# Cast order and block 0's gates in the opening, and the last P4 readout, of a fast-matrix-product ReGLU MLP

## The chip, the core and the metric

The kernel runs on one core of a Trainium2 chip. The metric is the device time of one execution in microseconds (us), median of several runs. TensorE (PE) multiplies, VectorE (DVE) and ScalarE (ACT) read its results out of PSUM and convert types, GpSimd (POOL) adds in SBUF, and DMAs are issued from the queues of SyncE (SP), POOL and ACT.

## The reference

```python
batch, seq, dim, hidden = 16, 256, 512, 2048
def reference(x, w1, w2):              # x [16,256,512], w1 [512,4096], w2 [2048,512], float32
    h = x @ w1
    gate, value = np.split(h, 2, axis=-1)
    h = np.maximum(gate, 0) * value
    return (h @ w2).astype(np.float32)
```

## The kernel before

**Tiling.** The 4096 rows of x are four sets of 1024 tokens; `w1` is 16 blocks of 128 hidden columns, each with a gate and a value part. All matmuls take float16 operands and add up in float32 in PSUM. The first product of a block is done by a scheme with seven products in place of eight (class `Block`, P1 to P7, two 512-wide matmuls each), on sums of blocks of x (`x_S1` to `x_S4`) and of `w1` (`wt`) that DVE and POOL make. The second product (`mm2_stream`) has the same seven steps for each of four groups `b` of 128 tokens per half set, eight 256-wide matmuls a step; it is woven into the next set's first product, and the last set's stands alone at the end. Its P4 ends a group: ACT reads 256 columns of the PSUM tile `Y` into the first half of `o2` (L333; the profile calls the tile `pv`), whose second half DVE wrote at P7 (L327), and a DMA carries them to the output (L337). In the last set, groups 2 and 3 send the two halves by DMAs of their own; P4's half goes out from the ACT queue for group 2 and from SP for group 3, the last of all.

**The opening (L417 to L486).** In set 0 the first three blocks are computed without the scheme, by class `Plain`: four accumulated matmuls (e = 0 to 3 over the 512 input columns) for a gate and four for a value. `whole[0..2]` are those blocks for the first 512 tokens, `parts` for the second 512 in two pieces of 256; `lead` is block 3, the first with the scheme. SP loads, in this order: two halves of the first tokens' x (`xf`), the weights of blocks 0 and 1 (all gates, then all values, `fetch_wl`), half of the next tokens (`xg`), block 2's gate weights, block 2's value weights, and the other half of `xg`. In the profile the float32 landing places carry the names of the tiles they borrow: x is `g_S`, the weights are `g`.

All waits come from the tile framework; the order on each engine is the program's order. PE runs `idle(NWARM)`, that is eight 512-wide matmuls on zeros (L177), then transposes x by `turn_pair` (L382; eight 128-wide ones a call). Of the two PSUM tiles of a call DVE copies one and ACT the other into `x_A` as float16 (L384). `cast_w(jb, g_)` (L397 to L400) casts one block's gate or value weights to float16 in `wr`, in two instructions: ACT takes e = 0, 1 and DVE e = 2, 3. The casts of block 0's gate weights stand between the two `turn_pair` calls in the program, so on ACT and DVE they are ahead of the copies of the second call. Block 0's gates are taken as two runs of four 256-wide matmuls, `gates((0,))` and `gates((1,))`, the first of which needs only the first 256 tokens.

For each block `close()` follows `values()`: ACT scales the value out of PSUM (L269), DVE multiplies it with the gate (L270). The second 512 tokens are cast to float16 by DVE in two instructions (L458 and L468, 1024 columns each), transposed on PE in float16 by `turn_half` (L390), and copied by DVE (L391). `cast_w(2, 0)` and `cast_w(2, 1)` are block 2's, at L462 and L465.

Of the kernel before, what the change touches and what calls it, by code (L numbers as in the profile page):

```python
# [11 lines left out]
MAX, MULT = mybir.AluOpType.max, mybir.AluOpType.mult  # L12
LE, GE, LT, ABS_MAX = (getattr(mybir.AluOpType, n) for n in ("is_le", "is_ge", "is_lt", "abs_max"))
COPY, SQUARE = mybir.ActivationFunctionType.Copy, mybir.ActivationFunctionType.Square
ENG = mybir.EngineType

P = 128
TH = 512
PERIOD = 7
NWARM = 8  # L20
NFILL = 1
NPLAIN = 3
HIGH, LOW = 512.0, 32.0
GS = 2.0 ** -19
SLOT = {"P1": 0, "P5": 1, "P2": 3, "P6": 4, "P3": 5, "P7": 9, "P4": 13}
HALF = 256
# [3 lines left out]
@with_exitstack  # L30
def kernel(ctx: ExitStack, tc: tile.TileContext, x, w1, w2, out):

    nc = tc.nc
    x2 = x.flatten_outer_dims()
    out2 = out.flatten_outer_dims()  # L40
    flagpool = ctx.enter_context(tc.tile_pool(name="flagpool", bufs=1))
    flag = flagpool.tile([1, 1], dt.int32, name="flag")
    with ExitStack() as fast:
        unfit = fast_way(fast, tc, x2, w1, w2, out2, flag)
    with tc.If(unfit > 0, label="general"):
        with ExitStack() as general:
            general_way(general, tc, x2, w1, w2, out2)
# [52 lines left out]
def fast_way(ctx, tc, x2, w1, w2, out2, flag):  # L100

    nc = tc.nc
# [7 lines left out]
    NB = TH // P  # L110
# [17 lines left out]
    place = {jb + i: (c, i) for c, (jb, n) in enumerate(CHUNKS) for i in range(n)}  # L128
    wr = [wpool.tile([P, 4, 2, n * P], F16, name=f"wr{c}") for c, (_, n) in enumerate(CHUNKS)]
# [44 lines left out]
    def idle(n):  # L174
        for _ in range(n):
            t = psy.tile([P, TH], F32, name="Y", tag="Y")
            nc.tensor.matmul(t, warm_b[:, :P], warm_b[:, :TH], start=True, stop=True)  # L177
# [106 lines left out]
    def mm2_stream(s, go):  # L284
        last = s == NS - 1
        S = {}

        def mm(name, b, ps, fresh):
            vn, gn = WX[name]
            for k in range(NHC):  # L290
                nc.tensor.matmul(ps, go[gn][:, k, b * P:(b + 1) * P], V[vn][:, k, :], start=fresh and k == 0,  # L291
                                 stop=k == NHC - 1, skip_group_check=True)
                if k < NHC - 1:
                    yield

        def take(pool, nm):
            return pool.tile([P, TH], F32, name=nm, tag=nm)[:, :HALF]

        def step(name, b):
            d = S.setdefault(b, {})  # L300
            if name == "P1":
                d["X"] = take(psx, "X")
                yield from mm("P1", b, d["X"], True)
                d["Y"] = take(psy, "Y")
                nc.scalar.copy(out=d["Y"], in_=d["X"])
            elif name == "P5":
                d["W"] = take(psw, "W")
                yield from mm("P5", b, d["W"], True)
                t = tmp.tile([P, 2, TH], F32, name="pv", tag="tmp")
                d["pu"], d["o2"] = t[:, 0].rearrange("p (a n) -> p a n", a=2), t[:, 1]  # L310
                nc.scalar.activation(d["pu"][:, 0], d["W"], COPY, scale=1 / GS)
            elif name == "P2":
                yield from mm("P2", b, d["X"], False)
                d["o1"] = tmp.tile([P, DO], F32, name="o", tag="o", bufs=4)
                nc.scalar.activation(d["o1"][:, :HALF], d["X"], COPY, scale=1 / GS)
            elif name == "P6":
                yield from mm("P6", b, d["Y"], False)
                nc.scalar.activation(d["pu"][:, 1], d["Y"], COPY, scale=-1 / GS)
            elif name == "P3":
                yield from mm("P3", b, d["W"], False)  # L320
                nc.vector.scalar_tensor_tensor(out=d["o1"][:, HALF:], in0=d["W"], scalar=1 / GS, in1=d["pu"][:, 1],  # L321
                                               op0=MULT, op1=ADD)
                for n in (slice(0, HALF), slice(HALF, DO)) if last and b >= 2 else (slice(0, DO),):
                    nc.sync.dma_start(out=out_v[s, 0, b, :, n], in_=d["o1"][:, n])
            elif name == "P7":
                yield from mm("P7", b, d["Y"], False)
                nc.vector.scalar_tensor_tensor(out=d["o2"][:, HALF:], in0=d["Y"], scalar=-1 / GS, in1=d["pu"][:, 0],  # L327
                                               op0=MULT, op1=ADD)
                if last and b >= NB - 2:
                    nc.sync.dma_start(out=out_v[s, 1, b, :, HALF:], in_=d["o2"][:, HALF:])  # L330
            else:
                yield from mm("P4", b, d["Y"], False)
                nc.scalar.activation(d["o2"][:, :HALF], d["Y"], COPY, scale=1 / GS)  # L333
                half = last and b >= NB - 2
                n = slice(0, HALF if half else DO)
                queue = nc.scalar if half and b == NB - 2 else nc.sync
                queue.dma_start(out=out_v[s, 1, b, :, n], in_=d["o2"][:, n])  # L337
            yield

        order = [("P1", 0), ("P1", 1), ("P1", 2), ("P2", 0), ("P2", 1), ("P2", 2)]  # L340
        order += [(n, b) for n in ("P5", "P6", "P3", "P7", "P4") for b in (0, 1)]
        order += [("P1", 3), ("P5", 2), ("P2", 3), ("P5", 3)]
        order += [(n, b) for n in ("P6", "P3", "P7", "P4") for b in (2, 3)]
        for i, (n, b) in enumerate(order):
            for f in BESIDE.get((s, i), ()):
                f()
            yield from step(n, b)
# [19 lines left out]
    def g_tiles():  # L367
# [5 lines left out]
    xf, xg = (go[n].rearrange("p a t -> p (a t)").bitcast(F32).rearrange("p (b d) -> p b d", b=NB) for n in ("S1", "S2"))  # L373
    xh = go["S4"][:, :NB]
    wl = [g[:, j0:j1].rearrange("p a t -> p (a t)").bitcast(F32).rearrange("p (e g j) -> p e g j", e=4, g=2)
          for j0, j1 in ((NJ - 4, NJ), (NJ - 6, NJ - 4))]

    def turn_pair(o, b0, pool, nm):
        for b in (b0, b0 + 1):
            ps = pool.tile([P, 4, P], F32, name=nm, tag=nm)  # L380
            for e in range(4):
                nc.tensor.transpose(ps[:, e], xf[:, b, e * P:(e + 1) * P], ident[F32])  # L382
            copy = nc.scalar.copy if b % 2 else nc.vector.tensor_copy
            copy(out=o["A1"][:, :, b * P:(b + 1) * P], in_=ps)  # L384

    def turn_half(o, b0, copy):
        ps = psx.tile([P, 4, 2, P], F16, name="X", tag="X")
        for b in range(2):
            for e in range(4):
                nc.tensor.transpose(ps[:, e, b], xh[:, b0 + b, e * P:(e + 1) * P], ident[F16])  # L390
        copy(out=o["A2"][:, :, b0 * P:(b0 + 2) * P], in_=ps.rearrange("p e b t -> p e (b t)"))  # L391

    def turn_by_dma(s, o, h):
        for k in range(2):
            nc.sync.dma_start_transpose(out=o[f"A{h + 1}{k + 1}"], in_=x16[s][h * TH:(h + 1) * TH, k * 256:k * 256 + 256])

    def cast_w(jb, g_):  # L397
        c, i = place[jb]
        for es, copy in ((slice(0, 2), nc.scalar.copy), (slice(2, 4), nc.vector.tensor_copy)):
            copy(out=wr[c][:, es, g_, i * P:(i + 1) * P], in_=wl[c][:, es, g_, i * P:(i + 1) * P])  # L400

    def fetch_wl(jb, g_, n=1):
        c, i = place[jb]
# [29 lines left out]
    whole = [Plain(g, jb, xo["A1"], 0, 0, 2) for jb in range(NPLAIN)]  # L433
# [12 lines left out]

    idle(NWARM)
    turn_pair(xo, 0, psw, "W")
    cast_w(0, 0)
    idle(NFILL)  # L450
    turn_pair(xo, 2, psx, "X")
    whole[0].gates((0,))
    cast_w(1, 0)
    whole[0].gates((1,))
    whole[1].gates(None, psy, "Y")
    cast_w(0, 1)
    cast_w(1, 1)
    nc.vector.tensor_copy(out=xh[:, :2], in_=xg[:, :2])  # L458
    whole[0].values()
    whole[0].close()  # L460
    whole[1].values()
    cast_w(2, 0)  # L462
    turn_half(xo, 0, nc.vector.tensor_copy)
    whole[2].gates(None, psy, "Y")
    cast_w(2, 1)  # L465
    whole[1].close()
    whole[2].values()
    nc.vector.tensor_copy(out=xh[:, 2:], in_=xg[:, 2:])  # L468
    whole[2].close()
    part(parts[0][0])  # L470
    turn_half(xo, 2, nc.vector.tensor_copy)
# [66 lines left out]
    for s in range(NS):  # L538
# [7 lines left out]
        last = NJ * PERIOD  # L546
# [16 lines left out]
        for at in range(first * PERIOD, last + PERIOD):  # L563
            if at in plan:
                jb, n = plan[at]
# [87 lines left out]
```

## Time and profile before

| what | value |
|---|---|
| median of 5 runs | 308.35 us (308.21 to 308.58) |
| the profiled execution | 308.04 us, of which the profile's span is 306.2 us |
| granted TensorE clock, mean | 0.999 |
| DVE busy | 219.1 us (72% of the span) |
| ACT busy | 189.7 us (62%) |
| POOL busy | 139.7 us (46%) |
| first 8.38 us: PE busy | 5.77 us |
| 8.38 to 22.00 us: PE / DVE / ACT busy | 13.62 / 11.36 / 7.44 us |
| 303.00 us to the end: PE busy | 0.00 us |

The span is the profiler's window of one execution; 1.84 us of the measured time lie around it. "Busy" is time in instructions, with the overlap of neighbours taken out. In the timeline a line gives the start, the duration, the engine (PEld is PE's weight load, SPq and ACTq are DMA issues), the line of the code, the operation and its tiles, and in brackets the idle time in front of it with what ended it. An "x8" is a merged run of eight.

### The profile page before, as it was taken

Reading aid. Unit: us, or ns where it says so; the run is one execution under the profiler, and the core shown is the slowest. Engines: PE = TensorE matmul, PEld = TensorE weight load, DVE = VectorE, ACT = ScalarE, POOL = GpSimd, SP = SyncE. Lnnn points to the kernel's source line nnn. Section 1 sums busy time; section 2 is a strip of 40 time slices with the busy share of each in tenths; the row PEclk is TensorE's granted clock in tenths of the full one; section 3 lists DMA queues with packets and bytes.
Section 4 is the critical chain, followed back from the end, with each engine's and each line's share of the span. In section 5 each row is a group of like instructions: output and inputs, shape, how many; then the busy total and the mean of one; then the engine's idle time right before and its main releaser. Section 6 shows DMA issues by size and latency. Waiting matters only on the chain.

```text
span 306.2 us, 5113 instructions
## 1 busy us (share of the span) xinstructions
PE 300.1 (98%) x1868; PEld 182.1 (59%) x1868; DVE 219.1 (72%) x346; ACT 189.7 (62%) x457; POOL 139.7 (46%) x127
## 2 busy tenths in 40 slices
PE   7999999999999999999999999999999999999995
PEld 3574444588844444478864444458884444447884
DVE  1798898896468888884347888886525888888502
ACT  2557776568576666737856767656857676763231
POOL 1749999810005448990002335995000434799000
PEclk9999999999999999999999999999999999999999
DMA  6999986989615740055130010027311101000123
GB/s 226 306 204 205 205 203 198 180 162 184 233 68 104 140 103 1 2 119 158 68 137 8 30 34 2 0 58 150 137 72 68 34 2 34 0 2 0 68 90 123
DMA packets 34410, 31.54 MB, mean 103 GB/s; under 512 B 14448, under 2 KB 28784, under 8 KB 34160
## 3 DMA queue, kind: packets, MB, share of 16 engines
q1 hardware_dynamic: 24608, 20.32, 22.0%
q0 software_dynamic: 9104, 10.75, 21.2%
q8 instruction: 15, 0.25, 0.3%
q10 hardware_dynamic: 672, 0.13, 0.2%
q14 instruction: 11, 0.09, 0.1%
HBM read 24.12 MB, written 11.53 MB: 116 GB/s over the span
## 4 chain that ended last, share of the span: by engine, by line
PE 96%; DMA 2%; ACT 0%; SPq 0%; issue 0%; ACTq 0%
PE Y L205 26%; PE X L205 17%; PE W L205 17%; PE Y L291 14%; PE X L291 9%; PE W L291 9%; DMA g<-in_w_dram 2%; PE W L255 2%; PE X L255 1%; PE Y L255 1%; SPq L418 0%; PE X L390 0%; ACT Y L212 0%; ACT wr L400 0%; ACT pv L333 0%
## 5 line engine op out<-in xcount | busy, mean ns | idle before, releaser
L280 POOL TENSOR_TENSOR g_S<-g 128x512 f16<-128x512 f16 (+1 forms) x46 | 58.1, 1290 | 126.3 <-DVE g L244 126.3
L205 PEld LDWEIGHTS <-wt 128*128 128x128 f16 x488 | 47.7, 98 | 55.8 <-issue 0.3
L205 PE MATMUL X<-x_A,wr 128*128 128x512 f16 x244 | 72.6, 379 | 0.1
L205 PE MATMUL Y<-x_S,wt 128*128 128x512 f16 x244 | 72.6, 379 | 0.0
L205 PEld LDWEIGHTS <-wr 128*128 128x128 f16 x366 | 35.8, 98 | 41.4 <-issue 0.4
L232 DVE SCALAR_TENSOR_TENSOR cc<-W,pu 128x512 f32<-128x512 f32 x61 | 42.2, 691 | 24.1 <-ACT pu L226 24.1
L212 ACT COPY Y<-X 128x512 f32<-128x512 f32 x61 | 34.8, 570 | 38.0 <-PE X L205 37.5
L291 PEld LDWEIGHTS <-g_S 128*128 128x128 f16 x512 | 50.0, 98 | 5.8
L238 DVE SCALAR_TENSOR_TENSOR cc<-Y,pu 128x512 f32<-128x512 f32 x61 | 42.1, 691 | 6.3
L226 ACT ACTIVATE pu<-Y 128x512 f32<-128x512 f32 x61 | 36.4, 596 | 13.9 <-PE Y L205 13.9
L233 DVE SCALAR_TENSOR_TENSOR g<-X,cc 128x512 f16<-128x512 f32 x61 | 42.2, 691 | 2.4
L244 DVE SCALAR_TENSOR_TENSOR g<-Y,cc 128x512 f16<-128x512 f32 x61 | 41.5, 680 | 1.8 <-PE Y L205 1.8
L291 PEld LDWEIGHTS <-g 128*128 128x128 f16 x384 | 37.6, 98 | 8.2
L219 ACT ACTIVATE pu<-W 128x512 f32<-128x512 f32 x61 | 36.8, 603 | 0.3 <-PE W L205 0.3
L205 PE MATMUL Y<-x_A,wt 128*128 128x512 f16 x122 | 36.3, 379 | 0.0
L205 PE MATMUL W<-x_S,wt 128*128 128x512 f16 x122 | 36.3, 379 | 0.0
L205 PE MATMUL W<-x_S,wr 128*128 128x512 f16 x122 | 36.3, 379 | 0.0
L291 PE MATMUL X<-w,g 128*128 128x256 f16 x256 | 31.2, 273 | 0.0
L291 PE MATMUL Y<-v,g_S 128*128 128x256 f16 x256 | 30.6, 273 | 0.0
L321 DVE SCALAR_TENSOR_TENSOR o<-W,pv 128x256 f32<-128x256 f32 x16 | 6.8, 424 | 29.5 <-PE W L291 29.5
L280 POOL TENSOR_TENSOR g_S<-g,g_S 128x512 f16<-128x512 f16 x18 | 21.8, 1209 | 1.4
L280 POOL TENSOR_TENSOR g_S<-g_S,g 128x512 f16<-128x512 f16 x18 | 20.8, 1155 | 1.4
(76 smaller groups left out, 284.4 us busy)
## 6 DMA issues: line engine op xcount, KB each, us to landing
out_dram<-o SPq DMA_DIRECT2D x14, 256.0 KB, 2.1
out_dram<-pv SPq DMA_DIRECT2D x14, 256.0 KB, 2.0
x<-in_x_dram POOLq DMA_DIRECT2D x3, 1024.0 KB, 9.0
xn<-x SPq DMA_DIRECT2D x12, 256.0 KB, 3.2
g_S<-in_x_dram SPq DMA_DIRECT2D x4, 512.0 KB, 6.4
wr<-in_w_dram POOLq DMA_DIRECT2D x4, 512.0 KB, 13.0
w<-in_w_dram POOLq DMA_DIRECT2D x4, 512.0 KB, 15.4
g<-in_w_dram SPq DMA_DIRECT2D x2, 512.0 KB, 6.4
```

Source lines behind the costliest of these rows:

```text
L205: nc.tensor.matmul(ps, W(wn, self.jb)[:, b], self.xo[xn][:, b, :], start=fresh and b == 0, stop=b == 1, skip_group_check=True)
L212: nc.scalar.copy(out=self.Y, in_=self.X)
L219: nc.scalar.activation(self.p5, self.W, COPY, scale=GS)
L226: nc.scalar.activation(self.u2, self.Y, COPY, scale=-GS)
L232: nc.vector.scalar_tensor_tensor(out=self.c12, in0=self.W, scalar=GS, in1=self.u2, op0=MULT, op1=ADD)
L233: nc.vector.scalar_tensor_tensor(out=self.g[:, self.jb, :TH], in0=self.X, scalar=0.0, in1=self.c12, op0=MAX, op1=MULT)
L238: nc.vector.scalar_tensor_tensor(out=self.c22, in0=self.Y, scalar=-GS, in1=self.p5, op0=MULT, op1=ADD)
L244: nc.vector.scalar_tensor_tensor(out=self.g[:, self.jb, TH:], in0=self.Y, scalar=0.0, in1=self.c22, op0=MAX, op1=MULT)
L255: nc.tensor.matmul(ps[:, ts], W(names[e // 2], self.jb)[:, e % 2], self.a[:, e, ts], start=e == 0, stop=e == 3, skip_group_check=True)
L280: eng.tensor_tensor(go[n][:, h0:h1], go[i0][:, h0:h1], go[i1][:, h0:h1], op=op)
L291: nc.tensor.matmul(ps, go[gn][:, k, b * P:(b + 1) * P], V[vn][:, k, :], start=fresh and k == 0, stop=k == NHC - 1, skip_group_check=True)
L321: nc.vector.scalar_tensor_tensor(out=d["o1"][:, HALF:], in0=d["W"], scalar=1 / GS, in1=d["pu"][:, 1], op0=MULT, op1=ADD)
```

## The change

The warm-up grows from eight to ten matmuls. Each cast of a block's weights is split into two calls, `cast_half`, and the halves change engines: DVE now takes e = 0, 1 and ACT e = 2, 3. Block 0's gate casts move behind the second `turn_pair`, and its gates become four 512-wide matmuls. Block 2's four half casts are spread out: DVE's stand ahead of block 0's multiply (gate weights) and ahead of the copy of `turn_half` (value weights), ACT's behind the value scaling of block 0 and of block 1. The cast of the second half of `xg` becomes two instructions of 512 columns. At the very last P4, group 3 of set 3, ACT reads columns 0 to 127 and DVE columns 128 to 255 of the same PSUM tile, by a multiplication with the same factor; every other P4 is as it was.

```diff
-NWARM = 8
+NWARM = 10
...
                 yield from mm("P4", b, d["Y"], False)
-                nc.scalar.activation(d["o2"][:, :HALF], d["Y"], COPY, scale=1 / GS)
                 half = last and b >= NB - 2
+                n = slice(0, P if last and b == NB - 1 else HALF)
+                nc.scalar.activation(d["o2"][:, n], d["Y"][:, n], COPY, scale=1 / GS)
+                if n.stop < HALF:
+                    nc.vector.tensor_scalar(out=d["o2"][:, P:HALF], in0=d["Y"][:, P:HALF], scalar1=1 / GS,
+                                            scalar2=None, op0=MULT)
                 n = slice(0, HALF if half else DO)
...
+    def cast_half(jb, g_, e0, copy):
+        c, i = place[jb]
+        es = slice(e0, e0 + 2)
+        copy(out=wr[c][:, es, g_, i * P:(i + 1) * P], in_=wl[c][:, es, g_, i * P:(i + 1) * P])
+
     def cast_w(jb, g_):
-        c, i = place[jb]
-        for es, copy in ((slice(0, 2), nc.scalar.copy), (slice(2, 4), nc.vector.tensor_copy)):
-            copy(out=wr[c][:, es, g_, i * P:(i + 1) * P], in_=wl[c][:, es, g_, i * P:(i + 1) * P])
+        cast_half(jb, g_, 0, nc.vector.tensor_copy)
+        cast_half(jb, g_, 2, nc.scalar.copy)
...
     idle(NWARM)
     turn_pair(xo, 0, psw, "W")
-    cast_w(0, 0)
     idle(NFILL)
     turn_pair(xo, 2, psx, "X")
-    whole[0].gates((0,))
+    cast_w(0, 0)
+    whole[0].gates()
     cast_w(1, 0)
-    whole[0].gates((1,))
     whole[1].gates(None, psy, "Y")
     cast_w(0, 1)
     cast_w(1, 1)
     nc.vector.tensor_copy(out=xh[:, :2], in_=xg[:, :2])
+    cast_half(2, 0, 2, nc.vector.tensor_copy)
     whole[0].values()
     whole[0].close()
     whole[1].values()
-    cast_w(2, 0)
+    cast_half(2, 0, 0, nc.scalar.copy)
+    cast_half(2, 1, 2, nc.vector.tensor_copy)
     turn_half(xo, 0, nc.vector.tensor_copy)
     whole[2].gates(None, psy, "Y")
-    cast_w(2, 1)
     whole[1].close()
+    cast_half(2, 1, 0, nc.scalar.copy)
     whole[2].values()
-    nc.vector.tensor_copy(out=xh[:, 2:], in_=xg[:, 2:])
+    for b in (2, 3):
+        nc.vector.tensor_copy(out=xh[:, b], in_=xg[:, b])
     whole[2].close()
```

## The prediction

> **What bounds the kernel.** I read the page first, then the chain that ended last, then the timeline of the opening and of the end.
>
> ```profile
> PE 300.1 (98%) x1868; PEld 182.1 (59%) x1868; DVE 219.1 (72%) x346; ACT 189.7 (62%) x457; POOL 139.7 (46%) x127
> ...
> PE 96%; DMA 2%; ACT 0%; SPq 0%; issue 0%; ACTq 0%
> ```
>
> PE is busy for 98% of the span and makes up 96% of the chain. From its first weight matmul at 8.38 us to 22.00 it is busy for all of 13.62 us, and afterwards it hardly stops. So two stretches alone can give time: the start, until PE runs without gaps, and the end, after PE's last matmul. A shift of PE in the opening is carried to the end, since PE has next to no idle time later that could swallow it.
>
> ```profile
> 1.28 3.59 PE L177 MATMUL Y<-warm 128*128 128x512 f16 x8 [1.28 <-DVE warm L167]
> ...
> 5.37 1.06 PE L382 MATMUL W<-ident,g_S 128*128 128x128 f32 x8 [0.50 <-DMA g_S<-in_x_dram]
> ...
> 6.49 1.06 PE L382 MATMUL X<-ident,g_S 128*128 128x128 f32 x8
> 7.92 0.41 ACT L400 CAST wr<-g 128x256 f16<-128x256 f32 x1 [0.86 <-DMA g<-in_w_dram]
> 7.92 0.29 DVE L400 CAST wr<-g 128x256 f16<-128x256 f32 x1 [1.19 <-DMA g<-in_w_dram]
> 8.13 0.68 DVE L384 CAST x_A<-X 128x512 f16<-128x512 f32 x1
> 8.23 0.58 ACT L384 CAST x_A<-X 128x512 f16<-128x512 f32 x1
> 8.38 0.33 PEld L255 LDWEIGHTS <-wr 128*128 128x128 f16 x4 [1.07 <-ACT wr L400]
> ...
> 9.31 1.03 PE L255 MATMUL Y<-x_A,wr 128*128 128x512 f16 x4
> ...
> 10.18 1.89 PE L255 MATMUL W<-x_A,wr 128*128 128x512 f16 x8
> ...
> 11.90 0.61 PE L390 MATMUL X<-ident,g_S 128*128 128x128 f16 x8
> ...
> 12.35 1.07 PE L255 MATMUL Y<-x_A,wr 128*128 128x512 f16 x4
> 12.48 0.28 DVE L400 CAST wr<-g 128x256 f16<-128x256 f32 x1
> 12.56 0.40 ACT L400 CAST wr<-g 128x256 f16<-128x256 f32 x1 [0.43 <-DMA g<-in_w_dram]
> ...
> 13.26 1.03 PE L255 MATMUL W<-x_A,wr 128*128 128x512 f16 x4
> ```
>
> The reader is to see that the weights land at about 7.9, that the slower cast (ACT, done 8.33) lets PE start at 8.38, 0.05 later, and that the copies of x wait behind the casts although their transposes had ended by 7.54. From then on the starts are 0.215 us apart for a 512-wide matmul (eight from 10.18 to 11.90).
>
> **The opening, step by step.** Pure PE work from the first gate to block 2's values is 4 x 0.215 for each of the three gates, 8 x 0.215 for two values and 0.45 (11.90 to 12.35) for the transposes: 4.75 us. Before, it took 13.26 - 8.38 = 4.88; the 0.13 over are small waits for the copies of x and for DVE's casts of block 2.
>
> After the change, the DVE copy follows the fourth transpose (about 7.09) and ends near 7.77; ACT's follows the eighth (7.54) and ends at 7.56 + 0.58 = 8.14. DVE's cast runs from 7.92 to 8.21, ACT's from about 8.04 (rows overlap by 0.1 here: 8.23 against 8.33) to 8.45. The gates' first two matmuls need all of x (8.14) and DVE's cast (8.21): they start at 8.21 + 0.05 = 8.26; the third, 0.43 later, finds ACT's cast done. Then PE goes through: block 1 at 9.12, block 0's values at 9.98 (weights landed by 9.40, casts done by 9.81), block 1's at 10.84, transposes at 11.70 (x cast from 10.80 to 11.49), block 2's gates at 12.15. Block 2's gate weights were issued at 3.58 and landed 8.1 later, 11.68; the ACT half ends at 11.70 + 0.40 = 12.10, the DVE half at 11.98: just in time. Its value weights landed at 12.53. On ACT the value scaling of block 1 now lies ahead of the cast: 12.00 to 12.60, then cast to 12.96, and PE is ready at 13.01. That is 0.25 under 13.26.
>
> The moved casts also block queues. On DVE the value-weight cast waits for 12.53 with the `turn_half` copy behind it, which then ends at about 13.5 (before 13.36); the first part's gates want it at 13.88. Split into two 512-column casts, each 0.42 (between 0.284 for 256 and 0.684 for 1024 columns), the second `xg` cast runs from 14.07 to 14.83, its first half done at 14.49; the transposes want them at 14.75 and 14.97. They cost nothing as long as that cover of 0.1 to 0.4 us holds. Swapped engines cost nothing: each still does six casts. No DMA is added in the opening, and none is passed by another.
>
> Two more warm matmuls: eight took 0.427 each, so at that rate ten end at 1.28 + 4.27 = 5.55, and the transposes, free at 5.37, start 0.18 late. ACT's copy of x then ends at 8.32 and the gates start at 8.37, which leaves 13.26 - (8.37 + 4.75) = 0.14 of gain. If the clock has risen by the ninth, they end by 5.13 and cost nothing. The rows only bound the rise: the eighth still took 0.63, while the filler at 6.27 was followed after 0.22. I take the middle, **-0.19**, with -0.14 and -0.25 as the ends.
>
> [...]
>
> **The end.**
>
> ```profile
> 302.86 0.38 ACT L333 ACTIVATE pv<-Y 128x256 f32<-128x256 f32 x1 [0.49 <-PE Y L291]
> 303.27 0.33 SPq L337 DMA_DIRECT2D out_dram<-pv  x1
> ```
>
> This pair is on the path: PE is done, and the DMA lands 2.0 later. ACT on 256 columns takes 0.383, on 512 0.600 (L219, L226), hence 128 take 0.383 - 0.108 = 0.275. DVE out of PSUM takes 0.424 for 256 and 0.691 for 512; 128 take 0.29. A smaller tensor_scalar, 128x88 in SBUF, took 0.198, so 0.24 is the lower end. If both read at once, the issue moves to 302.86 + 0.29 + 0.03 = 303.18: -0.09. If DVE follows ACT, 302.86 + 0.275 + 0.03 + 0.29 + 0.03 = 303.48: +0.21 (0.16 with 0.24). No row of before has ACT and DVE inside one PSUM tile at once: `Y` goes from ACT (L226, 22.03) to PE to DVE (L238, 23.99). That is the nearest row, so I take one after the other: **+0.21**.
>
> [...]
>
> **Sum.** -0.19 + 0.21 = +0.02. The profiled execution took 308.04 (306.2 span, 1.84 around it), so 308.06 of its kind; it lay 0.31 under the median, and on the median of 308.35 the sum gives **308.37**. A change under 0.2%, 0.62 us, is about what a measurement of this kernel can't tell from none.
>
> **Rivals.** *Both read at once*: the framework orders by columns, tail -0.09. For it: ACT and DVE write different parts of one SBUF tile together at 7.92. Against it: no such pair in PSUM. -0.19 - 0.09 gives 308.07. *ACT as the new gate of block 2*: its value cast now sits behind a 0.60 scaling, with 13.01 - 12.96 - 0.05, nothing, to spare. It costs what the cast ends past 12.96, and the opening as a whole is lost from 13.21 on. A whole scaling more (13.61) makes the opening +0.35, and with +0.21 the time 308.91. For it: the landing at 11.68 starts that chain, cast, scaling, cast. Against: the overlaps of 0.1 that ACT shows everywhere. *The opening does nothing*, because something later absorbs it: +0.21, 308.56; the page's 98% speaks against it, and I count it with the rest.
>
> **Numbers.** Forecast 0.60, both at once 0.22, ACT as gate 0.10, the rest 0.08. The likeliest one's own range is -0.09 to +0.07 with 0.15 for the spread of medians: 308.1 to 308.6. The range reaches down over the first rival (to -0.34, 308.01) and part of the way to the second: 307.95 to 308.70. Faster by 0.2% takes 0.02 of the first rival and 0.04 of the rest: 0.06; slower takes half of the second and 0.03 of the rest: 0.08; within: 0.86.
>
> **What would show it.** Right: gates from about 8.3, block 2's values between 13.0 and 13.1, PE gapless after, and at the end a DVE row of 0.24 to 0.29 that begins where ACT's 0.275 ends. Wrong: those two rows side by side; transposes not starting at 5.37 to 5.55; block 2's values after 13.26 with an ACT cast as releaser; or a new PE wait after 22 us, which none of my terms has.

## The result and the profile after

The changed kernel took 308.92 us (median of 27 runs, 308.48 to 309.83) against 308.32 for the kernel before in the same comparison (47 runs): a ratio of 1.0018, 95% interval 1.0012 to 1.0025. It is slower by 0.6 us, just under the 0.2% bound of the forecast and above its range. The prediction took a change under 0.2% for one that can hardly be told from none; with this many runs the interval lies clear of 1. The profiled execution took 309.02 us, with a span of 307.2.

The opening of the changed kernel, from the timeline (start, duration, engine, line, operation):

```profile
1.28 4.45 PE L177 MATMUL Y<-warm 128*128 128x512 f16 x10 [1.28 <-DVE warm L167]
...
5.52 1.62 PE L386 MATMUL W<-ident,g_S 128*128 128x128 f32 x8
...
7.20 1.04 PE L386 MATMUL X<-ident,g_S 128*128 128x128 f32 x8
...
8.27 0.59 ACT L388 CAST x_A<-X 128x512 f16<-128x512 f32 x1 [0.50 <-PE X L386]
...
8.91 1.02 PE L255 MATMUL X<-x_A,wr 128*128 128x512 f16 x4 [0.67 <-ACT x_A L388]
...
13.67 1.03 PE L255 MATMUL W<-x_A,wr 128*128 128x512 f16 x4
```

The ten warm-up matmuls end as the worst case had them, and the transposes start at 5.52. But the first eight take 1.62 us where they took 1.06: up to 6.59 they start 0.21 us apart, after that 0.11, as all of them did before. The trace's record of the full granted clock begins at 6.71 us here and at 5.29 in the profile of before; ahead of it PE runs at half speed (the warm-up matmuls start 0.43 us apart, 512-wide ones later 0.215). The last copy of x therefore ends at 8.86, 0.72 later than the 8.14 of the forecast (0.54 later than its 8.32 for a late clock), and the gates wait for it. The chain of waits shows the same in one piece:

```profile
5.30 0.43 PE Y L177
5.73 1.42 PE W L386 x8
7.14 0.22 PE Y L177
7.36 0.89 PE X L386 x8
8.25 0.02 issue
8.27 0.59 ACT x_A L388
8.87 0.04 issue
8.91 0.81 PE X L255 x3
```

Before, the chain ran over the landing of the weights at 7.89 and their cast; now warm-up, transposes and a copy of x lead to the first gate. Block 2's values start at 13.67, 0.41 later than before (0.05 of it because the weights landed at 7.94 and not 7.89), and PE ends 0.40 later (303.22 against 302.82).

The end, from the timeline:

```profile
303.26 0.28 ACT L335 ACTIVATE pv<-Y 128x128 f32<-128x128 f32 x1 [0.49 <-PE Y L291]
303.57 0.29 DVE L337 TENSOR_SCALAR pv<-Y 128x128 f32<-128x128 f32 x1 [1.63 <-ACT pv L335]
303.89 0.33 SPq L341 DMA_DIRECT2D out_dram<-pv  x1
```

VectorE starts 0.03 after ScalarE ends, so the two reads are one after the other, and the DMA is issued 0.63 after ScalarE's start instead of 0.41. The list of DMA issues around that point gives its time to landing (last column), before and after:

```profile
out_dram<-pv SPq DMA_DIRECT2D x1, 128.0 KB, 2.0
```

```profile
out_dram<-pv SPq DMA_DIRECT2D x1, 128.0 KB, 2.4
```

By the trace's landings it is 2.01 and 2.38. So the profiled spans (306.25 and 307.23, 0.98 apart) divide by stages into 0.40 opening, 0.22 readout and 0.37 landing. What caused the last two is another question, for the experiments.

### The profile page after: what moved, and what is told of

It is laid out like the page before. It is cut to its first block, busy times and chain, and to the rows that moved or that the text cites. A ratio compares the mean times of both kernels' runs of the same rounds, so it can differ in the third digit from the quotient of the medians.

```text
span 307.2 us, 5111 instructions
## 1 busy us (share of the span) xinstructions
PE 301.1 (98%) x1866; PEld 182.9 (60%) x1866; DVE 219.9 (72%) x348; ACT 189.7 (62%) x457; POOL 139.7 (45%) x127
## 4 chain that ended last, share of the span: by engine, by line
PE 98%; ACT 0%; issue 0%; DVE 0%; DVEq 0%; ACTq 0%
PE Y L205 26%; PE X L205 17%; PE W L205 17%; PE Y L291 14%; PE X L291 9%; PE W L291 9%; PE W L255 2%; PE Y L177 2%; PE X L255 1%; PE Y L255 1%; PE W L386 0%; PE X L394 0%; PE X L386 0%; ACT x_A L388 0%; ACT Y L212 0%
```

## The experiments

In each comparison the kernel before ran on the same chip. Single executions of one kernel spread over 0.5 us and more there, so beside the median the lowest run is given; both are differences to the kernel before of the same comparison. "Fetch" is where VectorE's last instruction fetch (8192 bytes on the DMA queue q14; counted as VectorE's because it follows VectorE's closing branch by 1.19 to 1.29 us in every trace) begins, counted from the issue of the last output DMA; that issue is also where "landing" is counted from. The kernel before has two to three times as many runs as an experiment, which alone puts its lowest run a little lower.

| kernel | median | lowest | ratio, 95% interval | issue after ScalarE's start | fetch | landing |
|---|---|---|---|---|---|---|
| before (profile) | | | | 0.41 | -0.95 | 2.01 |
| after | +0.60 | +0.41 | 1.0012 to 1.0025 | 0.63 | +0.89 | 2.38 |
| e1 tail alone | +0.45 | +0.50 | 0.9997 to 1.0039 | 0.63 | +0.89 | 2.36 |
| e6 ScalarE twice | -0.20 | +0.04 | 0.9978 to 1.0008 | 0.47 | -1.02 | 1.96 |
| e7 two tiles | +0.69 | +0.68 | 1.0001 to 1.0038 | 0.42 | +0.85 | 2.66 |
| e5 late VectorE | -0.20 | -0.11 | 0.9981 to 1.0014 | 0.41 | +1.31 | 2.01 |
| e9 VectorE timed | -0.19 | -0.02 | 0.9974 to 1.0012 | 0.41 | +0.62 | 2.07 |
| e10 split and more | +0.64 | +0.64 | 1.0006 to 1.0046 | 0.63 | +0.91 | 2.77 |
| e13 fetch in the way | +0.38 | +0.57 | 0.9988 to 1.0022 | 0.46 | +1.00 | 2.45 |
| e16 its control | +0.18 | +0.03 | 0.9976 to 1.0013 | 0.47 | -1.01 | 1.97 |
| e14 split, fetch later | 0.00 | +0.10 | 0.9987 to 1.0026 | 0.63 | +1.48 | 1.77 |

**Which part costs: e1 and e2.** e1 is the kernel before with the tail's edit alone, e2 the changed kernel without it.

> The kernel before with only the last P4's readout split between ScalarE and VectorE. Theory A (the two reads of one PSUM tile go one after the other): the ScalarE row of about 0.28 ends before the VectorE row of 0.29 begins, the last DMA is issued 0.63 us after ScalarE's start instead of 0.41, and the median rises by 0.2 us, somewhat more if the landing of that DMA (2.0 before, 2.4 in the changed kernel) has to do with the split. Rival B (the split does nothing, all 0.6 us come from the opening): no change in the median within 0.1 us.

> The changed kernel with the last P4 read by ScalarE alone, as before; only the opening differs from the kernel before. Theory A (opening about +0.4, because the float32 transposes run at half clock until it rises, at 5.29 us in the profile of before and 6.71 in that of after, and their copies are now ahead of the casts): median +0.3 to +0.5 us, and in the profile the start of block 0's gates follows the moment of the rise, 8.3 if it rises by 5.4 and 8.9 if at 6.7. Rival B (the opening gains 0.19 as forecast and the tail loses all of it and more): median -0.1 to -0.25 us.

e1 rose by 0.45 us, with ScalarE's row, VectorE's row and the issue spaced as in the changed kernel. e2 had the median of before, 308.65 against 308.66 (ratio 1.0, 0.9981 to 1.0018), neither the +0.4 of theory A nor the gain of rival B; in its profile the clock rose at 6.18 and the gates began at 8.65. So by median and by lowest run (+0.50 and +0.11) the loss is the tail's, and it is more than the later issue explains. The intervals of the two overlap; the kernels below bear the reading out.

**Why the reads are in order: e7.** The last group's second 128 columns get a PSUM tile of their own.

```diff
+        def mm_two(b, d):
...
+            for k, i in [(k, i) for k in range(NHC) for i in range(2)]:
+                nc.tensor.matmul((d["Y"][:, :P], d["Z"])[i], go[gn][:, k, b * P:(b + 1) * P], V[vn][:, k, i * P:(i + 1) * P],
+                                 start=False, stop=k == NHC - 1, skip_group_check=True)
...
+                if last and b == NB - 1:
+                    d["Z"] = take(psy, "Y")[:, :P]
+                    nc.scalar.copy(out=d["Z"], in_=d["Y"][:, P:HALF])
...
```

> The last P4's columns 128 to 255 are accumulated in a PSUM tile of their own (ScalarE copies the partial sums there after P7; 16 matmuls of 128 columns in place of 8 of 256, in turns), and ScalarE and VectorE read one tile each. Theory A (it is the shared PSUM tile that puts the reads one behind the other): the two rows lie side by side, the DMA is issued 0.32 us after PE's end instead of 0.63, but VectorE's late fetch still costs the landing; median +0.1 to +0.3 over before. Rival B (the two engines are put in order by the shared output tile): VectorE's row still begins after ScalarE's ends.

```profile
304.51 0.28 ACT L346 ACTIVATE pv<-Y 128x128 f32<-128x128 f32 x1 [0.59 <-PE Y L299]
304.57 0.29 DVE L348 TENSOR_SCALAR pv<-Y 128x128 f32<-128x128 f32 x1 [1.48 <-PE Y L299]
304.93 0.33 SPq L352 DMA_DIRECT2D out_dram<-pv  x1
```

Both rows now wait for PE and lie side by side, though they still write one SBUF tile: it was the shared PSUM tile that put them in order (VectorE starts 0.06 us after ScalarE here, 0.31 after it in the changed kernel). What two reads of one PSUM tile at once would do, no trace shows. The time did not improve (+0.69). Part of that is PE's own: with the sixteen narrow matmuls and the copy ahead of them it ends 0.15 later, counted from block 2's values (289.71 against 289.56 before). The landing took 2.66 in this profile, of which more below.

**Where the landing goes: e6, e5, e9, e10.** e6 keeps two readouts of 128 columns, both by ScalarE. e5 adds one VectorE copy of a column that nothing waits for. e9 and e10 add more VectorE work, to place its end earlier (e9, on the kernel before) or later (e10, on the split).

```diff
+                for n in (slice(0, P), slice(P, HALF)) if last and b == NB - 1 else (slice(0, HALF),):   # e6
+                    nc.scalar.activation(d["o2"][:, n], d["Y"][:, n], COPY, scale=1 / GS)
...
+                    nc.vector.tensor_copy(out=gate, in_=d["o2"][:, :1])                                  # e5
...
+                    nc.vector.tensor_tensor(t[2], t[0], t[1], op=ADD)                                    # e9, e10
+                    nc.vector.tensor_copy(out=gate, in_=d["o2"][:, :1])
```

> The last P4 read by ScalarE alone, in two instructions of 128 columns. Theory A (a late VectorE costs the landing, the hand-over between engines the rest): the DMA is issued 0.5 us after ScalarE's start, against 0.41 before and 0.63 with the split, VectorE's fetch lies at 302.3 to 302.5 as before, and the median rises by about 0.1 us only, against 0.45 for the split. Rival B (any later issue of the last DMA costs more than its delay): 0.3 us or more.

> The kernel before, whole, plus one VectorE copy of a single column per partition that reads what ScalarE wrote for the last P4 and that nothing waits for. Theory A (the last VectorE instruction decides when VectorE's closing instruction fetch of 8192 bytes runs; in the two kernels with the split it began 1.2 us after that instruction, at 304.78 and 304.47, among the packets of the last output DMA, and that DMA landed 2.38 and 2.36 us after its issue instead of 2.01): the DMA is issued at the same point as before (0.41 after ScalarE's start), the fetch begins about 1.2 us after the copy, the landing takes 2.2 to 2.5 us, and the median rises by 0.1 to 0.4 us. Rival B (the landing varies by itself): fetch as said, but landing 2.0 and no change of the median.

> The kernel before, plus three VectorE instructions at the end on data that nobody uses, set so that VectorE's last one begins about 0.3 us ahead of the last DMA's issue, as with the split; nothing on the path changes. Theory A (VectorE's closing instruction fetch, 1.2 us after its last instruction starts, delays the last DMA when it falls 0.9 us after that DMA's issue, as at 304.78 and 304.47 with the split; 1.3 us after it, as with the late copy, it came too late to do so): issue as before, fetch 0.8 to 1.0 us after it, landing 2.3 to 2.7 us, median +0.2 to +0.4. Rival B (landings of 2.4 are chance): landing 2.0 in the profile and median within 0.1 us of before.

> The readout split as in the changed kernel, on the kernel before, plus two further VectorE instructions behind it on data that nobody uses, which move VectorE's end about 0.6 us later. Theory A: the DMA is issued 0.63 us after ScalarE's start as with the split alone, the fetch falls 1.4 to 1.6 us after that issue, out of the way, the DMA lands in 2.0 to 2.1 us, and the kernel is 0.2 to 0.4 us faster than the split alone: +0.2 over before, with more work. Rival B (chance, or the split itself): as slow as the split alone, +0.45.

e6 costs nothing that can be measured, so a readout in two pieces is not the point. e5, e9 and e10 all missed their aim: the fetch began at +1.31, +0.62 and +0.91 from the issue, and the medians were nearer to their rivals B than to their theories A. The fetch follows VectorE's closing branch by 1.19 to 1.29 us in all eighteen traces (301.13 to 302.32 before, 303.58 to 304.78 after), and the branch can come ahead of the last instruction's start (e10: branch at 303.39, last copy at 303.97). By where the fetch really fell they agree: at +0.91 the landing took 2.77, at +0.62 and +1.31 it took 2.07 and 2.01. That reading was made after the fact, so two more kernels were aimed with it.

**The fetch in the way, and out of it: e13, e16, e14.** e16 reads with ScalarE alone, in 64 and 192 columns; e13 adds a VectorE copy of one column that waits for the first of these. e14 keeps the changed kernel's split and adds a ScalarE copy and a VectorE copy behind it, so that VectorE ends later.

```diff
+                for n in (slice(0, 64), slice(64, HALF)) if last and b == NB - 1 else (slice(0, HALF),):  # e13, e16
+                    nc.scalar.activation(d["o2"][:, n], d["Y"][:, n], COPY, scale=1 / GS)
+                if last and b == NB - 1:                                                                  # e13
+                    nc.vector.tensor_copy(out=gate, in_=d["o2"][:, :1])
...
+                    nc.scalar.copy(out=t[:, :512], in_=t[:, 512:])                                        # e14
+                    nc.vector.tensor_copy(out=gate, in_=t[:, :1])
```

> The last P4 read by ScalarE alone in two instructions, 64 and 192 columns, and one VectorE copy of one column that waits for the first of them and that nothing waits for. Theory A (VectorE's closing fetch, 1.2 us after its last wait ends, delays the last output DMA when it begins some 0.9 us after that DMA's issue): fetch 0.85 to 1.0 us after the issue, landing 2.3 to 2.8 us after it, and 0.2 to 0.5 us slower than the same kernel without the copy (e16). Rival B (the long landings have another cause): landing 2.0 to 2.1, no difference from e16 above 0.1 us.

> The same two ScalarE instructions, 64 and 192 columns, without the VectorE copy. Both theories: the DMA is issued 0.45 to 0.5 us after ScalarE's start, VectorE's fetch lies near 302.4 as before, landing 2.0 to 2.1 (2.4 where TensorE's own fetch is long), median 0 to 0.1 us over before.

> The readout split as in the changed kernel, on the kernel before, and behind it a ScalarE copy of 512 columns on data nobody uses and a VectorE copy of one column that waits for it, so that VectorE's end comes some 0.5 us later. Theory A: the fetch begins 1.3 us or more after the last DMA's issue, which lands in 2.0 to 2.1 us; 0.2 to 0.3 us slower than before, and 0.2 to 0.3 faster than the split alone, though it does more. Rival B: 0.4 to 0.6 us slower than before, like the split alone.

The end of e14 shows the split as in the changed kernel, with the extra work beside and behind it, and the time to landing:

```profile
303.02 0.28 ACT L335 ACTIVATE pv<-Y 128x128 f32<-128x128 f32 x1 [0.49 <-PE Y L291]
...
303.33 0.29 DVE L337 TENSOR_SCALAR pv<-Y 128x128 f32<-128x128 f32 x1 [1.63 <-ACT pv L335]
303.65 0.33 SPq L344 DMA_DIRECT2D out_dram<-pv  x1
303.84 0.15 DVE L341 CAST gate<-x_S 128x1 f32<-128x1 f16 x1 [0.21 <-ACT x_S L340]
```

```profile
out_dram<-pv SPq DMA_DIRECT2D x1, 128.0 KB, 1.8
```

The list of DMA queues (packets, MB, share of 16 engines), for the changed kernel from 304.7 to 305.5 us and for e14 from 305.1 to 305.6; q14 carries the fetch, and 5.0% of sixteen engines' 0.8 us is 0.64 us:

```profile
q1 hardware_dynamic: 137, 0.12, 46.0%
q14 instruction: 1, 0.01, 5.0%
```

```profile
DMA packets 1, 0.01 MB, mean 16 GB/s; under 512 B 0, under 2 KB 0, under 8 KB 0
...
q14 instruction: 1, 0.01, 5.5%
```

In the changed kernel the fetch runs while 137 packets of the output move; it begins at 304.78 and takes 0.64 us, and the last eight output packets of 1 KB follow one by one from 305.42, when it is done. Fifteen of the DMA's sixteen parts had landed by 305.73; the sixteenth came at 306.27. In e14 the fetch begins at 305.13, when no output packet is left, and the DMA lands 1.77 after its issue. With the same split and two more instructions, e14's lowest run is 0.10 above before, where e1's is 0.50; its median is that of before. That is better than the 0.2 to 0.3 over before that theory A expected, and its landing shorter than the 2.0 to 2.1 expected. e13 puts the fetch at +1.00 without touching the issue: 2.45 against 1.97 in its control, lowest run 308.77 against 308.23. The medians differ by 0.20 only (309.02 and 308.82; the intervals overlap, and the control's +0.18 over before is itself outside the 0 to 0.1 expected), so the size rests on the lowest runs and on the profiles. All five kernels with the fetch 0.85 to 1.00 after the issue landed in 2.36 to 2.77, with lowest runs 0.41 to 0.68 over before; the five others of the table landed in 1.77 to 2.07, at -0.11 to +0.10. Of the 75 runs of the first five none lies within 0.40 us of the lowest run of before in its comparison; of the 60 of the others 33 do, and of the 175 of before 91 (the 0.40 was chosen with the numbers known).

**What the landing follows otherwise.** Kernels with the tail of before landed late too: e3 and e4 below in 2.43 and 2.44, e8 in 2.12, e15 in 2.23. There is another fetch, of 16384 bytes on the queue q8, which begins at about PE's end. Before, it is listed from 302.3 to 302.9 us with VectorE's (9.9% is 0.95 us):

```profile
q8 instruction: 1, 0.02, 9.9%
q14 instruction: 1, 0.01, 6.9%
```

In twelve of the eighteen traces the last DMA landed 1.49 to 1.60 us after the end of that fetch: in before, e2 to e9 and e14 to e16. The fetch took 0.88 to 0.95 us in the kernels of the table that landed in 1.77 to 2.07, and 1.33 and 1.31 in e3 and e4. It took 1.33 in e7 as well, whose landing it can account for without VectorE's fetch. In the four others with VectorE's fetch among the packets (after, e1, e10, e13) the landing came 1.88 to 2.45 after q8's end, 0.3 to 0.9 more; in e11 and e12, whose q8 fetch began before PE's end and took 1.61 and 1.68, it came 1.82 after it and 2.84 after the issue.

So by these traces the last issue did not set the landing of the kernel before. From ScalarE's start to the landing it takes 2.42 before, 2.43 in e6 and 2.40 in e14, which issues 0.22 later. That is, the later issue costs next to nothing, and VectorE's fetch nearly all of the tail's 0.59. No run moved the q8 fetch on purpose, so what it does to the landing is read from the traces and not shown by an experiment, and the landings of the other executions are not on record.

**The opening: e3, e4, e11, e12.** e3 is e2 with eight warm-up matmuls, e4 the kernel before with ten. e11 (changed opening) and e12 (opening of before) hold all loads back until ten warm-up matmuls are done and put 18 more behind them, so that the clock is up when x lands (eight transposes took 1.06 and 1.09 us in both); they ran once each, for the profile.

```diff
+    nc.vector.tensor_copy(out=held, in_=idle(10)[:, :1])
+    nc.sync.dma_start(out=x16[1][:P, :1], in_=held)
     for b in (0, 2):
         nc.sync.dma_start(out=xf[:, b:b + 2], in_=x_v[0, :, b:b + 2])
```

> The opening alone, with eight warm-up matmuls as before. Theory A (what counts is when the clock rises, and that is not set by two more matmuls): the median stays within 0.2 us of the opening alone with ten, and gates start where the rise puts them. Rival B (the ten matmuls delay the transposes by 0.18 us and that is the loss): 0.15 to 0.2 us faster than with ten, transposes from 5.37. Rival C (eight leave PE idle from 4.9 to 5.4 and the rise comes later): slower than with ten by up to 0.5 us.

> The kernel before with ten warm-up matmuls and nothing else. Theory A: the transposes have about 0.8 us to spare ahead of the casts, so the time stays within 0.15 us of before, at whatever moment the clock rises. Rival B (ten matmuls as such are the loss): +0.2 to +0.4 us.

> The changed opening (tail as before) with all loads held back until ten warm-up matmuls are done, and 18 more behind them, so that the clock is up before x lands; everything is some 5 us later. Read: block 2's values from the landing of the first weights. Theory A (only the slow transposes spoil the opening): 5.1 to 5.2 us after it, 0.25 less than the opening of before in the same test, as forecast. Rival B (the order as such gains nothing): 5.35 or more.

> The opening of before, with the same held-back loads and warm-up. Theory A and rival B both: block 2's values 5.37 us after the first weights land, as in the profiles of before with the clock rising at 4.7 to 6.5 us.

Block 2's values, counted from the landing of the first weights, against the moment at which the granted clock rose:

| opening | rise at, us | values after landing, us |
|---|---|---|
| before (profile, e1, e4, e5, e6, e9, e10) | 5.29, 4.67, 5.69, 6.45, 5.00, 5.47, 5.59 | 5.37, 5.37, 5.37, 5.36, 5.36, 5.37, 5.37 |
| before (e14) | 7.08 | 5.45 |
| before (e7, e13, e16) | 9.38, 10.68, 9.80 | 6.76, 6.79, 6.75 |
| before, clock up (e12) | ahead of the loads | 5.37 |
| changed (after, e2, e3) | 6.71, 6.18, 6.71 | 5.73, 5.48, 5.66 |
| changed, clock up (e11) | ahead of the loads | 5.15 |

The order of before does not feel the rise up to 6.45, and loses 0.08 at 7.08 and 1.4 at 9.4 to 10.7; the changed order gains 0.22 with the clock up and loses 0.1 to 0.4 where it rises after 6.1. Ten or eight warm-up matmuls make no such difference: e3's median is 308.69 against 308.65 for e2, and e4's lies 0.14 under before (0.9967 to 1.0005), so by the medians rival B of each fell. The line that decides in e11 and in e12:

```profile
13.45 1.04 PE L256 MATMUL X<-x_A,wr 128*128 128x512 f16 x4 [0.75 <-DVE wr L401]
```

```profile
13.86 1.10 PE L256 MATMUL X<-x_A,wr 128*128 128x256 f16 x8 [0.85 <-ACT wr L401]
```

With the weights at 13.08 and 13.37 the gates start 0.37 and 0.49 later, as the forecast had it for both orders, and the cast of the weights releases them, not the copy of x as in the changed kernel's own profile. Of the 0.22, 0.15 are left at PE's end (294.78 and 294.93 after the landing).

**A version between: e8, e15.** Both keep the swapped engines and the spread casts of block 2, with block 0's casts back ahead of the second transposes, its gates in two halves and the tail of before; e15 has ten warm-up matmuls and the x cast in one piece.

> The changed opening with eight warm-up matmuls, but block 0's casts back ahead of the second pair of transposes and its gates in two halves again; the tail as before. What stays of the change: the swapped engines, the spread casts of block 2, the split cast of x. Theory A (the opening loses by the copies of x that it puts ahead of the casts, when the clock rises late): block 2's values start 5.2 to 5.3 us after the first weights land, wherever the clock rises up to 6.8, against 5.37 before and 5.73 in the changed kernel; median 0.05 to 0.15 us under before. Rival B (the spread casts of block 2 are what costs): 5.4 us or more, not faster than before.

> A version meant to beat both: block 0's casts ahead of the second pair of transposes as before, engines swapped and block 2's casts spread as in the change, the x cast in one piece, the tail as before, ten warm-up matmuls so that PE has no gap before the transposes. Theory A: block 2's values 5.25 to 5.35 us after the first weights land at any rise up to 6.8, no executions above 309.5 us, median 0.05 to 0.25 us under before. Rival B (the warm-up makes no difference to the rise): slow executions above 309.5 as often as before, median as before.

e8: values at 5.32 after the landing, just outside what was expected, and no gain (308.45 against 308.43). e15: 5.33 with the rise at 6.52, median 308.48 (308.31 to 309.19, so none above 309.5, as expected) against 308.64, ratio 0.999, interval 0.9974 to 1.0006. It is faster than the changed kernel by these medians, but not shown to be faster than before.

## Why the prediction was wrong

- **The end, the readout.** The rows were right: 0.28 and 0.29 one after the other, issue +0.22 for the forecast +0.21. The rival "both read at once" fell (after, e1), and e7 shows why. But that the whole grows by what the issue loses was assumed, and e14 does not bear it out: issue +0.22, landing 0.02 earlier counted from ScalarE's start, median 0.00, lowest run +0.10.
- **The end, the landing.** This is the step that failed: "This pair is on the path: PE is done, and the DMA lands 2.0 later". The 2.0 was carried over as a constant, counted from the issue. Giving VectorE the last readout also moved VectorE's end, and its closing fetch, from 302.32, ahead of the last output DMA, to 304.78, among its packets. The landing took 2.38, against 1.77 with the same split and the fetch out of the way (e14). The tail costs 0.59 in the profile, 0.45 in the median and 0.50 in the lowest run of e1. That the fetch does it is shown by e14 and e13 against e16 in profiles and lowest runs, not in the intervals of the medians.
- **The opening.** The mechanism was right, and the term was mis-sized. With the clock up it gave -0.22 at block 2's values, within the -0.14 to -0.25 given. But the bound for a late clock counted the two longer warm-up matmuls (0.18) and not the transposes behind them, eight of which take 1.62 in place of 1.06 in the changed kernel; the rise at 6.71 cost 0.36, counted from the weights' landing, instead of leaving 0.14. Over e2's twelve executions gains and losses came to nothing in the median (0.0), with an interval of nearly 0.6 us either way.
- **The x cast in two at nothing.** Nearly: in e11, where PE is early, the transposes behind it take 0.69 instead of 0.61; that is part of the 0.07 lost between block 2's values and PE's end.
- **The rival with ACT as gate** did not come: in the changed kernel block 2's values start 0.87 after its gates (12.80 to 13.67), no more than four matmuls 0.215 apart need. That its 308.91 lies next to the measured 308.92 is chance.
- **PE without new waits after 22 us** held: PE's lag is 0.40 at block 3 (19.78 against 19.38) and 0.40 at PE's end.

By stages the sum +0.02 lacked 0.37 for the landing, and the opening's 0.19 did not come in e2's median: 0.21 + 0.37 is 0.58, next to the measured 0.60. By causes, e14 puts nearly all of the 0.58 on the fetch and next to nothing on the later issue.

## What to carry to other kernels

An engine that is handed the last piece of work also ends last, and what the program does when it ends can move with it (here VectorE's branch from 301.13 to 303.58 us, its instruction fetch from 302.32 to 304.78): look at what the closing DMAs meet. The time from a DMA's issue to its landing is no constant to carry over: here it ran from 1.77 to 2.84 us for the same 128 KB. A reordering that takes slack from work at a clock that may not be up yet must be priced at the slow clock, for all of that work (here a transpose every 0.21 us instead of 0.11). One profile shows one moment of the rise, which lay anywhere from 4.67 to 10.68 us in these; ask where another would put the chain.

## What the runs showed of the hardware

- The stretch at full granted clock lasted 296.96, 300.37 or 307.20 us in the eighteen traces (300.37 in the profiles of before and after), lengths 3.41 and 6.83 us apart. The rise fell anywhere from 4.67 to 7.08, in e7, e13 and e16 from 9.38 to 10.68. What sets the lengths is not shown.
- With eight warm-up matmuls PE idles between the last of them (4.87) and the transposes. In e7, e13 and e16 that gap was 0.64 to 0.69 us, and the clock rose only at 9.38 to 10.68; in e3, e5 and e14 it was 0.49 to 0.58, and the clock rose at 6.45 to 7.08. The gap alone does not decide, though: in e10 it was 0.66 and the clock rose at 5.59, in e6 0.64 and the clock rose at 5.00. What does is not shown. From e13's timeline, with both runs of eight transposes at half clock (1.94 and 1.91 us against 1.06 before):

```profile
5.51 1.94 PE L385 MATMUL W<-ident,g_S 128*128 128x128 f32 x8 [0.64 <-DMA g_S<-in_x_dram]
...
7.67 1.91 PE L385 MATMUL X<-ident,g_S 128*128 128x128 f32 x8
9.38 1.68 PE L255 MATMUL X<-x_A,wr 128*128 128x256 f16 x8
```

  There the gates begin 0.8 us late even in the order of before (1.33 after the weights' landing at 8.05, against 0.49 in e12), and block 2's values 1.4 us late. Of the executions of the kernel before in all comparisons, 21 of 175 lay above 309.7 us; of e2, e4 and e15, with ten warm-up matmuls and the tail of before, none of 36. That ten prevent the late rise fits this. e4 has that edit alone, but at 21 in 175 twelve executions would show none about one time in five, so it is not shown.
